# A batched matrix product in bf16: plain fp32 loads with casts on VectorE, stores on a second queue, long runs per partition

## The chip, the cores and the metric

The kernel runs on one core of a Trainium2 chip, with the other cores idle. Times are device microseconds of one execution. The profiled execution of the kernel before has a span of 276.1 us, while its timed executions have spans of 274.1 to 277.7 us (times 275.9 to 279.5), so it is one of its longer ones by about 1.7 us.

In the profiles PE is TensorE (matmuls), PEld its weight loads, DVE VectorE, ACT ScalarE, POOL GpSimd and SP SyncE; a q after a name is that engine's sequencer, which issues transfers and waits. SBUF is the on-chip memory with 128 partitions; PSUM takes the results of matmuls. A run is a piece of data that is contiguous in memory, and a packet is one record of a DMA engine's work.

## The reference

```python
batch, m, k, n = 16, 512, 768, 1024          # x: (16, 768, 512), y: (16, 768, 1024), fp32
np.einsum('bkm,bkn->bmn', x, y)              # out: (16, 512, 1024), fp32
```

It reads 75.5 MB and writes 33.55 MB, whatever the kernel does. Per batch, that is 4.72 MB in and 2.10 MB out.

## The kernel before

The load is a DMA on the GpSimd queue that casts fp32 to bf16 on its way. Row `ko*128 + p` of x or y goes to partition p, so a contiguous run is one row: 2 KB of x, 4 KB of y.

```python
x_v = x.rearrange("b (ko p) m -> b ko p m", p=P)
y_v = y.rearrange("b (ko p) n -> b ko p n", p=P)
o_v = out.rearrange("b (mo p) n -> b mo p n", p=P)
# x_pool, y_pool: 4 buffers; o_pool: 12; psum: 8 banks
for b in range(B):
    ...
    for c in range(LOAD_SPLIT):                       # two halves of the contraction
        ks = slice(c * KC, (c + 1) * KC)
        nc.gpsimd.dma_start(x_sb[:, ks], x_v[b, ks].rearrange("ko p m -> p ko m"))
        nc.gpsimd.dma_start(y_sb[:, ks], y_v[b, ks].rearrange("ko p n -> p ko n"))
    ...
    for kt in range(KT):                              # contraction outermost, 8 banks open
        for mt in range(MT):
            for nt in range(NT):
                mm(ps[mt * NT + nt], x_sb, y_sb, kt, mt, nt)
    for mt in range(MT):                              # copies alternate VectorE, ScalarE
        ...
        nc.sync.dma_start(o_v[b, mt], o_sb[mt][:])    # four stores of 512 KB
```

Of the kernel before, what the change touches and what calls it, by code (L numbers as in the profile page):

```python
# [1 line left out]

_os.environ.setdefault("NEURON_RT_ULTRASERVER_MODE", "4")

# [1 line left out]

# [4 lines left out]

LOAD_SPLIT = 2
K_OUTER = True


@with_exitstack
def kernel(
    ctx: ExitStack,
    tc: tile.TileContext,  # L20
    x: bass.AP,
    y: bass.AP,
    out: bass.AP,
):
    nc = tc.nc
    P = 128
    FP32 = mybir.dt.float32
    BF16 = mybir.dt.bfloat16

    B, K, M = x.shape  # L30
    _, _, N = y.shape

    KT = K // P
    MT = M // P
    NF = 512
    NT = N // NF
    KC = KT // LOAD_SPLIT

    x_v = x.rearrange("b (ko p) m -> b ko p m", p=P)
    y_v = y.rearrange("b (ko p) n -> b ko p n", p=P)  # L40
    o_v = out.rearrange("b (mo p) n -> b mo p n", p=P)

    x_pool = ctx.enter_context(tc.tile_pool(name="x_pool", bufs=4))
    y_pool = ctx.enter_context(tc.tile_pool(name="y_pool", bufs=4))
    o_pool = ctx.enter_context(tc.tile_pool(name="o_pool", bufs=12))
    psum = ctx.enter_context(tc.tile_pool(name="psum", bufs=8, space=bass.MemoryType.PSUM))

    def mm(ps, x_sb, y_sb, kt, mt, nt):
        nc.tensor.matmul(  # L49
            ps[:],  # L50
            x_sb[:, kt, mt * P:(mt + 1) * P],
            y_sb[:, kt, nt * NF:(nt + 1) * NF],
            start=(kt == 0),
            stop=(kt == KT - 1),
        )

    for b in range(B):
        x_sb = x_pool.tile([P, KT, M], BF16, name="x_sb")
        y_sb = y_pool.tile([P, KT, N], BF16, name="y_sb")
        for c in range(LOAD_SPLIT):  # L60
            ks = slice(c * KC, (c + 1) * KC)
            nc.gpsimd.dma_start(  # L62
                x_sb[:, ks], x_v[b, ks].rearrange("ko p m -> p ko m"))
            nc.gpsimd.dma_start(  # L64
                y_sb[:, ks], y_v[b, ks].rearrange("ko p n -> p ko n"))

        o_sb = [o_pool.tile([P, N], FP32, name="o_sb") for _ in range(MT)]
        ps = [psum.tile([P, NF], FP32, name="ps") for _ in range(MT * NT)]
        if K_OUTER:
            for kt in range(KT):  # L70
                for mt in range(MT):
                    for nt in range(NT):
                        mm(ps[mt * NT + nt], x_sb, y_sb, kt, mt, nt)
            for mt in range(MT):
                for nt in range(NT):
                    j = mt * NT + nt
                    eng = nc.vector.tensor_copy if j % 2 == 0 else nc.scalar.copy
                    eng(o_sb[mt][:, nt * NF:(nt + 1) * NF], ps[j][:])  # L78
                nc.sync.dma_start(o_v[b, mt], o_sb[mt][:])
        else:  # L80
            for mt in range(MT):
                for nt in range(NT):
                    j = mt * NT + nt
                    for kt in range(KT):
                        mm(ps[j], x_sb, y_sb, kt, mt, nt)
                    eng = nc.vector.tensor_copy if j % 2 == 0 else nc.scalar.copy
                    eng(o_sb[mt][:, nt * NF:(nt + 1) * NF], ps[j][:])
                nc.sync.dma_start(o_v[b, mt], o_sb[mt][:])


# [1 line left out]
_INS = ['x', 'y']  # L92
_OUTS = [((16, 512, 1024), 'float32')]


# [23 lines left out]
```

## Time and profile before

| | before |
|---|---|
| time, median | 276.1 us |
| PE busy | 192.3 us, 70% |
| DMA row of the page | 9 of 10 in all but the two ends |
| bytes at the source | 109.05 MB |
| from the last load's landing to the end of the span | 12.2 us |

The prediction below shows the page's lines. Here are the groups of instructions that the change touches. Columns: line, engine, operation, tiles, shapes, count; then busy us and mean ns of one; then the engine's idle time before them and what ended it.

```profile
L49 PE MATMUL ps<-y_sb,x_sb 128*128 128x512 bf16 x753 | 192.3, 416 | 77.0 <-DMA y_sb<-in_y_dram 72.3
L78 ACT COPY o_sb<-ps 128x512 f32<-128x512 f32 x64 | 32.9, 600 | 235.2 <-issue 172.9
L64 POOL DMA_DIRECT2D y_sb<-in_y_dram x32 | 24.7, 773 | 105.2 <-DMA y_sb<-in_y_dram 105.2
```

No engine but the DMA engines is full, and PE's idle time before matmuls ends with the landing of a load.

### The profile page before, as it was taken

The page shows a single profiled execution, that of the slowest core. Times are in us where ns is not written, and L with a number is a line of the kernel's source. Part 1 is how long each engine was busy: PE and PEld are TensorE (multiplying, and loading weights), DVE is VectorE, ACT ScalarE, POOL GpSimd, SP SyncE. Part 2 cuts the span into 40 slices and gives each one's busy share as a digit, 9 for nine tenths or more (in the row PEclk, how much of TensorE's full clock was granted, in tenths as well). Part 3 has the DMA queues.
Part 4 walks back from the last instruction along what each step waited for, and adds up shares of the span by engine and source line. Part 5 has one row for each costly group of instructions (what it writes and reads, how often), then busy time and mean ns, then how long its engine had stood idle before and what let it go on. Part 6 is the DMA issues. An engine that isn't in the chain of part 4 may idle for free.

```text
span 276.1 us, 2127 instructions
## 1 busy us (share of the span) xinstructions
PE 192.3 (70%) x753; PEld 79.9 (29%) x768; DVE 39.7 (14%) x64; ACT 34.1 (12%) x65; POOL 49.8 (18%) x68
## 2 busy tenths in 40 slices
PE   0599727698278788495784993769919695849770
PEld 0144313243133333132331441324403332313330
DVE  0003110033003003030300303003030030302011
ACT  1002110022002002020200202002020020202011
POOL 8422121221212122121212311122112221000000
PEclk9999977799689979889978898689986998997997
DMA  5999999999999999999999999999999999999937
GB/s 92 202 208 237 317 279 284 208 243 315 296 268 210 284 279 245 315 210 297 260 294 267 211 302 286 319 216 209 320 291 302 209 252 309 223 315 233 283 156 304
DMA packets 34826, 71.44 MB, mean 259 GB/s; under 512 B 2048, under 2 KB 14336, under 8 KB 34816
## 3 DMA queue, kind: packets, MB, share of 16 engines
q0 software_dynamic: 25600, 37.75, 75.7%
q1 hardware_dynamic: 9216, 33.56, 32.2%
q8 instruction: 6, 0.10, 0.1%
q14 instruction: 4, 0.03, 0.0%
HBM read 75.50 MB, written 33.55 MB: 395 GB/s over the span
## 4 chain that ended last, share of the span: by engine, by line
DMA 90%; issue 3%; POOL 2%; PE 2%; DVE 0%; DVEq 0%; POOLq 0%
DMA x_sb<-in_x_dram 78%; DMA y_sb<-in_y_dram 12%; PE ps L49 2%; POOL x_sb L62 1%; POOL y_sb L64 1%; DVE o_sb L78 0%; DVEq L114 0%; DVEq L78 0%; POOLq L114 0%; POOLq L103 0%
## 5 line engine op out<-in xcount | busy, mean ns | idle before, releaser
L49 PE MATMUL ps<-y_sb,x_sb 128*128 128x512 bf16 x753 | 192.3, 416 | 77.0 <-DMA y_sb<-in_y_dram 72.3
L49 PEld LDWEIGHTS <-x_sb 128*128 128x128 bf16 x768 | 79.9, 105 | 188.8 <-issue 109.9
L78 DVE COPY o_sb<-ps 128x512 f32<-128x512 f32 x64 | 39.7, 683 | 230.6 <-issue 167.7
L78 ACT COPY o_sb<-ps 128x512 f32<-128x512 f32 x64 | 32.9, 600 | 235.2 <-issue 172.9
L64 POOL DMA_DIRECT2D y_sb<-in_y_dram x32 | 24.7, 773 | 105.2 <-DMA y_sb<-in_y_dram 105.2
L62 POOL DMA_DIRECT2D x_sb<-in_x_dram x32 | 24.8, 777 | 76.5 <-DMA x_sb<-in_x_dram 70.7
L78 ACT ACT_TABLE_LOAD x1 | 1.3, 1283 | 0.7 <-PEq L103 0.7
L103 POOL MEMSET const-float32-0.0<- 128x1 f32 x1 | 0.1, 93 | 0.2 <-issue 0.2
L103 POOL MEMSET const-bfloat16-1.0<- 128x1 bf16 x1 | 0.1, 95 | 0.0
L103 POOL MEMSET const-float32-1.0<- 128x1 f32 x1 | 0.1, 93 | 0.0
L103 POOL MEMSET const-uint8-127<- 128x1 uint8 x1 | 0.1, 93 | 0.0
## 6 DMA issues: line engine op xcount, KB each, us to landing
out_dram<-o_sb SPq DMA_DIRECT2D x64, 512.0 KB, 8.9
y_sb<-in_y_dram POOLq DMA_DIRECT2D x32, 768.0 KB, 32.9
x_sb<-in_x_dram POOLq DMA_DIRECT2D x32, 384.0 KB, 32.8
```

The costliest lines, as they stand in the source:

```text
L49: nc.tensor.matmul(ps[:], x_sb[:, kt, mt * P:(mt + 1) * P], y_sb[:, kt, nt * NF:(nt + 1) * NF], start=(kt == 0), stop=(kt == KT - 1),)
L62: nc.gpsimd.dma_start(x_sb[:, ks], x_v[b, ks].rearrange("ko p m -> p ko m"))
L64: nc.gpsimd.dma_start(y_sb[:, ks], y_v[b, ks].rearrange("ko p n -> p ko n"))
L78: eng(o_sb[mt][:, nt * NF:(nt + 1) * NF], ps[j][:])
L103: nc = _bacc.Bacc("TRN2", target_bir_lowering=False, num_devices=1)
```

## The change

The intent is to take the cast off the DMA and GpSimd off the loads: plain copies on a hardware queue, with rows so long that each partition reads one contiguous piece. Row `p*6 + ko` now goes to partition p, so a run is 12 KB of x and 24 KB of y; output row `p*4 + mo` makes a store run 16 KB. VectorE casts from a staging buffer, and ScalarE alone empties PSUM. The order of instructions is fixed by hand (`tc.manual_schedule()`), and x and y have 2 bf16 buffers instead of 4. The diff, cut to its core:

```diff
-    x_v = x.rearrange("b (ko p) m -> b ko p m", p=P)
-    y_v = y.rearrange("b (ko p) n -> b ko p n", p=P)
-    o_v = out.rearrange("b (mo p) n -> b mo p n", p=P)
+    x_v = x.rearrange("b (p ko) m -> b p ko m", ko=KT)
+    y_v = y.rearrange("b (p ko) n -> b p ko n", ko=KT)
+    o_v = out.rearrange("b (p mo) n -> b p mo n", mo=MT)
...
+    def store(b):
+        nc.scalar.dma_start(o_v[b], o_tiles.pop(b)[:])
...
-            nc.gpsimd.dma_start(x_sb[:, ks], ...)     # two halves, cast in the DMA
-            nc.gpsimd.dma_start(y_sb[:, ks], ...)
+            nc.sync.dma_start(xs[:], x_v[b])          # fp32, staging, 2 buffers
+            nc.sync.dma_start(ys[:], y_v[b])
+            if False:
+                store(b - LAG)                        # LAG = 4, switched off
...
+            nc.vector.tensor_copy(x_sb[:], xs[:])
+            for h in range(2):
+                ks = slice(h * KT // 2, (h + 1) * KT // 2)
+                nc.vector.tensor_copy(y_sb[:, ks], ys[:, ks])
+            x_w = x_sb[:].rearrange("p k (j mo) -> p k mo j", mo=MT)   # weights stepped by 4
...
+            for mo in range(MT):                      # contraction innermost
+                for nt in range(NT):
+                    for kt in range(KT):
+                        nc.tensor.matmul(ps[:], x_w[:, kt, mo], y_sb[:, kt, ns], ...)
+                    nc.scalar.copy(o_sb[:, mo, ns], ps[:])
+            if True:
+                store(b)                              # one store of 2 MB
```

## The prediction

> **What bounds the kernel now.** I read the page first (busy shares, DMA row, queues, chain), then the chain in order of time, then windows, then the timeline of the end.
>
> ```profile
> PE 192.3 (70%) x753; PEld 79.9 (29%) x768; DVE 39.7 (14%) x64; ACT 34.1 (12%) x65; POOL 49.8 (18%) x68
> ...
> DMA  5999999999999999999999999999999999999937
> ...
> q0 software_dynamic: 25600, 37.75, 75.7%
> q1 hardware_dynamic: 9216, 33.56, 32.2%
> ...
> HBM read 75.50 MB, written 33.55 MB: 395 GB/s over the span
> ...
> DMA 90%; issue 3%; POOL 2%; PE 2%; DVE 0%; DVEq 0%; POOLq 0%
> ```
>
> The DMA row shows 9 in 37 of 40 slices, the chain that ended last is 90% DMA, and the largest engine, PE, is busy for 70%. The kernel is bound by the 16 DMA engines for all but its two ends. q0 counts 37.75 MB because the page counts bytes at the destination, which is bf16 for loads; the source read 75.50 MB.
>
> At what rate do they run? Windows (engine columns first; granted clock, DMA share and GB/s at the end of a row):
>
> ```profile
> 48.00:58.00 10.00, 7.50 (x27) 3.06 (x27) 1.95 (x4) 1.73 (x4) 2.32 (x3) 0.83 1.17 209
> 28.00:32.00 4.00, 2.73 (x13) 1.27 (x13) 0.00 (x0) 0.00 (x0) 0.77 (x1) 1.00 1.10 330
> ...
> 4.00:264.00 260.00, 187.10 (x731) 77.75 (x746) 37.24 (x60) 30.80 (x60) 46.80 (x61) 0.89 1.12 265
> ...
> 264.00:276.00 12.00, 5.18 (x23) 2.14 (x22) 2.48 (x4) 2.05 (x4) 0.00 (x0) 0.87 0.52 206
> ```
>
> At 48 to 58 only loads run: 209 GB/s of bf16 landed is 418 GB/s of fp32 read. At 28 to 32 stores take the larger part. Over 4 to 264 us 265 x 260 = 68.9 MB landed; 37.75 of it is loads, so 31.15 MB is stores, and counted at the source 75.5 + 31.15 = 106.65 MB moved in 260 us, 410 GB/s. If loads cost what they cost alone, they take 75.5 / 0.418 = 180.6 us, leaving 79.4 us for 31.15 MB of stores, 392 GB/s. So the engines have no idle time to win, only rate: 418 for loads in rows of 2 and 4 KB, 392 for stores in rows of 4 KB.
>
> The end is the other term:
>
> ```profile
> 230.94 32.91 DMA y_sb<-in_y_dram
> 263.85 0.04 issue
> 263.89 2.53 PE ps L49 x11
> ...
> 263.89 5.34 PE L49 MATMUL ps<-y_sb,x_sb 128*128 128x512 bf16 x23 [3.08 <-DMA y_sb<-in_y_dram]
> ...
> 268.63 2.88 SPq L79 DMA_DIRECT2D out_dram<-o_sb  x4
> ```
>
> The last load lands at 263.85. Only half a batch, 24 matmuls, is left (5.34 us, 222 ns each), the copies follow with the last groups, and the first of four stores is issued at 268.63. From the last landing to the end it is 276.1 - 263.9 = 12.2 us. From the packet records, those four stores' packets begin 1.6 us after the first issue and move their 2.1 MB in 5.2 us.
>
> **What the Trainium skill says.** "DMA: Bandwidth & Descriptors", section Measured: one 16 MB load reaches 425 GB/s on a core alone, and section Where 436 GB/s comes from: 435 GB/s is the ports' ceiling. The trace agrees so far as 418 and 392 both lie below it. The same page, section Why small descriptors are slow: each packet carries a fixed overhead on the engine's internal bus. The trace hints at it: a 4 KB store row takes 4096 / (392/16) = 167 ns of one engine, against 151 ns at 435/16. "VectorE: DVE Perf Modes", section The perf-mode tier table: an fp32 copy of 2048 columns in SBUF takes 1227 ns, two results a cycle; nothing in this trace shows it, as VectorE here only reads PSUM (683 ns for 512 columns). "TensorE: Matmul & The Clock Gate", section Weight-path perf modes: the fast weight load stays available with a column step from -1,023 to 1,024; the changed kernel steps by 4. The trace shows only step 1, at 105 ns.
>
> **The change, part by part.**
>
> 1. Loads move from GpSimd with a cast to 32 plain loads on SP. The 64 GpSimd issues (49.5 us busy in all) vanish, but none but the first was on a path that mattered, since DMA was busy throughout: 0 us. HBM traffic is unchanged, 75.5 + 33.55 = 109.05 MB. A partition's rows become 12, 24 and (stores) 16 KB in one run instead of 2 and 4 KB. I expect the per-packet loss nearly to vanish: about 427 GB/s for everything, an estimate between the skill's 425 for one long load and its ceiling of 435.
>
> 2. Are the engines kept fed? A load of batch b+2 waits for the casts of b, about 5 us after b lands, while b+1 (4.72 MB, at least 11 us) is still queued. In the compiled order some loads also wait for a store's shared semaphore, one that belongs to a batch five earlier, long landed. So no gap.
>
> 3. VectorE casts: three of 128x3072 per batch; at the skill's rate 3072/2 cycles at 0.96 GHz plus the 160 ns left over of 1227: 1.76 us each, 5.3 us per batch. At one result a cycle it would be 3.4 us each, 10 us per batch. A batch lasts 6.82 MB / 0.427 = 16 us, so both lie beside the DMA, except in the last batch.
>
> 4. Copies all on ScalarE: 8 x 600 ns = 4.8 us per batch, beside the matmuls. PE: 48 x 222 ns = 10.7 us, some 12 with cold stretches (446 ns each after idle of 4.9 us in this trace), under 16. Both off the path but for the last batch.
>
> 5. The last batch is the cost. y is now one load per batch, not two halves, so all 48 matmuls wait for it, with its two casts ahead; the 2.1 MB store is one transfer after all eight copies. From the last landing: two casts 3.5 (three matmuls fit beside the second), 45 matmuls x 222 = 10.0, cold start 0.8, last copy with its waits 0.9, issue 0.3, first byte 1.6, 2.1 MB at 420 GB/s 5.0, closing 0.7: 22.8 us, against 12.2.
>
> Sum: the first load issues at about 0.9 and flows by 2.7 us. When the last load lands, 14 stores have gone: store 14 is issued about one batch (casts 3.5, matmuls 11.5, copy 0.7) after its load, just as load 15 lands. So 75.5 + 14 x 2.097 = 104.9 MB / 0.427 = 245.7 us; 2.7 + 245.7 = 248.4 for the last landing, 15.5 us earlier than now. Plus 22.8 gives 271.2, a little under 2% faster. The change wins about 15 us of rate and gives 10.6 back in the end. I write 271.5.
>
> **The rivals.**
>
> A: the rate does not rise. If the hardware cuts a long run back into 4 KB packets, loads stay near 418 and stores near 392, mix 410: 104.9 / 0.410 = 255.9, total 281, 2% slower. For it: the engines are already at 94% of the ceiling. Against it: stores and loads differ, and the stores' 16 ns a row is what a fixed packet cost looks like.
>
> B: PE becomes the bound. Weights stepped by 4 columns may load more slowly. [...]At 300 ns the batch takes 14.4 us, still hidden, and only the end pays 3.5 us: 275. At 430 ns it takes 20.6 us, and 16 of them plus 14 us of start give some 350. The present pitch of 222 ns with loads of 98 to 105 leaves room of a factor two; I give the slow form 4%.
>
> C: everything goes well: 432 GB/s (242.8 us), warm PE, first store bytes sooner: 267.
>
> D: VectorE casts at one result a cycle: only the end pays, 3.3 us: 275.
>
> **Range and chances.** Each 5 GB/s is 2.9 us. 420 to 432 GB/s spans 276 to 268 with the end as computed; the end itself may be off by 3 us either way. Two per cent faster is 270.6, which lies beside my centre and needs 428 or a shorter end; 2% slower is 281.6, which needs A in full, or B. I say 266 to 281, faster 0.43, same 0.48, slower 0.09.
>
> **What will show it.** Step 1: rows of 12 to 24 KB on both hardware queues, and packets of that size; a window in mid-kernel at 420 to 432 GB/s (now bytes landed equal bytes read). 4 KB packets at 400 to 410 would be A. Step 2: the DMA row at 9 from the second slice to about the 37th, and the SP issues never the last to be waited for by the engines. Step 3: the cast rows at about 1.76 us. Step 4: weight loads at 100 to 150 ns and a warm matmul pitch near 222; PE idle a few us in each batch waiting for VectorE. Step 5: last landing near 248 and some 23 us from there to the end, with DMA idle for part of it. The prediction is wrong if the mid-kernel rate is outside 415 to 435, if the DMA row has holes, or if the end differs from 23 us by more than 4.

## The result, and the profile after

The changed kernel takes 272.49 us (271.82 to 273.49, four runs) beside 276.17 us. The ratio is 0.9862 (0.9828 to 0.9895), so it is 1.4% faster. A ratio here is the mean time of one kernel's runs over that of the other's of the same rounds, so it is not quite the ratio of the medians. Executions over 1.5% slower than the fastest of the same kernel are left out of the means.

The page after: busy shares, the DMA row with its rates in 40 slices, the queues, the total and the chain.

```profile
PE 197.6 (73%) x768; PEld 89.8 (33%) x768; DVE 83.0 (31%) x48; ACT 76.4 (28%) x129; POOL 0.2 (0%) x4
...
DMA  7999999999999999999999999999999999996507
GB/s 290 421 446 419 433 349 439 421 435 444 417 438 428 430 433 438 429 418 447 419 438 421 434 442 410 451 424 439 422 426 430 422 441 436 430 434 268 237 0 309
...
q1 hardware_dynamic: 4608, 75.50, 65.6%
q10 hardware_dynamic: 2304, 33.56, 29.0%
...
HBM read 75.50 MB, written 33.55 MB: 402 GB/s over the span
...
DMA 82%; DVE 10%; PE 4%; DVEq 1%; SPq 0%; issue 0%; ACT 0%
```

The middle runs at 410 to 450 GB/s; bytes landed are now bytes read. The new thing is at the right: the DMA row ends 6 5 0 7. One slice of 6.8 us moves nothing at all.

Only loads run from 5 to 24 us in both kernels. The windows, first of the kernel before, then of the changed one:

```profile
5.00:24.00 19.00, 13.95 (x56) 6.08 (x58) 2.48 (x4) 2.05 (x4) 7.28 (x11) 1.00 1.15 205
```

```profile
5.00:24.00 19.00, 7.60 (x22) 3.02 (x23) 6.95 (x4) 1.76 (x3) 0.00 (x0) 1.00 1.02 437
```

205 GB/s of bf16 landed are 410 GB/s read; the changed kernel reads 437. (A window counts a packet where it starts, so a long packet can carry it a little past the true rate; single microseconds of the packet records give 430 to 433.)

The groups after, for the casts, the copies and PE:

```profile
L74 PE MATMUL ps<-y_sb,x_sb 128*128 128x512 bf16 x768 | 197.6, 420 | 65.8 <-DVE y_sb L65 65.8
L74 PEld LDWEIGHTS <-x_sb 128*128 128x128 bf16 x768 | 89.8, 119 | 173.1 <-issue 54.0
L76 ACT COPY o_sb<-ps 128x512 f32<-128x512 f32 x128 | 75.2, 587 | 186.8 <-PE ps L74 186.8
L65 DVE CAST y_sb<-ys 128x3072 bf16<-128x3072 f32 x32 | 54.9, 1757 | 140.0 <-DMA ys<-in_y_dram 140.0
```

The end of the chain in order of time (start, us, what), and the same stretch in windows:

```profile
221.17 28.02 DMA ys<-in_y_dram
...
249.28 1.76 DVE y_sb L65
251.04 1.68 DVEq L106
...
252.76 10.61 PE ps L74 x45
...
263.40 0.59 ACT o_sb L76
```

```profile
252.00:256.00 4.00, 3.81 (x14) 1.55 (x13) 0.71 (x1) 0.96 (x2) 0.00 (x0) 0.72 0.66 274
256.00:260.00 4.00, 4.00 (x21) 2.08 (x19) 0.00 (x0) 1.88 (x4) 0.00 (x0) 1.00 0.00 0
260.00:264.00 4.00, 3.36 (x16) 1.55 (x14) 0.00 (x0) 1.86 (x4) 0.00 (x0) 1.00 0.00 0
264.00:268.00 4.00, 0.00 (x0) 0.00 (x0) 0.00 (x0) 0.00 (x0) 0.00 (x0) 0.99 0.84 356
```

The last load lands at 249.2. Two casts, 45 matmuls and a copy follow one after the other. The store of the batch before is done by about 256, and then the DMA engines stand still until the last 2 MB are ready at 264.

From the packet records I worked out, for every run, the stretch from the first load packet to the last, the rate in it, the stores still to do at its end, and how long no DMA engine worked after it. Times are medians of the fast runs; all other columns are of one execution. This table carries the rest of the document.

| run (profiled execution) | first to last load, us | GB/s in it | stores left, MB | after it, us | of that no DMA at all, us | time, us |
|---|---|---|---|---|---|---|
| kernel before | 260.5 | 408 | 2.8 | 11.5 | 3.6 | 276.2 |
| changed kernel | 247.0 | 424 | 4.2 | 21.2 | 10.6 | 272.5 |
| e1_short_rows | 256.8 | 408 | 4.2 | 22.1 | 11.4 | 284.3 |
| e2_short_loads | 258.1 | 406 | 4.2 | 22.5 | 12.2 | 285.3 |
| e3_short_stores | 238.5 | 424 | 8.0 | 20.8 | 0.0 | 264.2 |
| e7_before_long_loads | 253.0 | 416 | 3.8 | 11.5 | 1.3 | 270.3 |
| e4_one_queue | 243.0 | 425 | 5.7 | 22.4 | 6.9 | 270.2 |
| e5_last_stores | 245.8 | 426 | 4.3 | 18.7 | 7.3 | 269.9 |
| e6_short_end | 247.0 | 424 | 4.2 | 15.5 | 3.1 | 267.5 |
| f3_packets_4k | 249.3 | 418 | 4.8 | 21.0 | 7.4 | 273.2 |
| f4_packets_8k | 243.1 | 426 | 5.5 | 22.5 | 7.6 | 270.2 |
| f5_padded | 239.9 | 425 | 7.2 | 21.1 | 0.3 | 265.8 |
| f1_lag4 | 232.8 | 427 | 9.7 | 24.3 | 0.0 | 261.9 |
| f2_lag4_short_end | 232.8 | 426 | 9.9 | 24.4 | 0.0 | 262.2 |

Here the change won 13.5 us of stream (260.5 to 247.0) and gave back 9.7 us after the last load (11.5 to 21.2). What is left, 3.8 us, and loads that start 1.1 us earlier (1.7 instead of 2.85 us) make the 5.0 us between the two spans. The times differ by 3.7, because the profiled execution of the kernel before was one of its longer ones.

### The profile page after: what moved, and what is told of

It reads as the page before. It is cut to its first block, busy times and chain, and to the rows that moved or that the text cites. A ratio compares the mean times of both kernels' runs of the same rounds, so it can differ in the third digit from the quotient of the medians.

```text
span 271.1 us, 1889 instructions
## 1 busy us (share of the span) xinstructions
PE 197.6 (73%) x768; PEld 89.8 (33%) x768; DVE 83.0 (31%) x48; ACT 76.4 (28%) x129; POOL 0.2 (0%) x4
## 4 chain that ended last, share of the span: by engine, by line
DMA 82%; DVE 10%; PE 4%; DVEq 1%; SPq 0%; issue 0%; ACT 0%
DMA ys<-in_y_dram 82%; DVE y_sb L65 10%; PE ps L74 4%; DVEq L106 1%; SPq L56 0%; ACT o_sb L76 0%; SPq L57 0%; DVEq L65 0%
## 5 line engine op out<-in xcount | busy, mean ns | idle before, releaser
L74 PE MATMUL ps<-y_sb,x_sb 128*128 128x512 bf16 x768 | 197.6, 420 | 65.8 <-DVE y_sb L65 65.8
L74 PEld LDWEIGHTS <-x_sb 128*128 128x128 bf16 x768 | 89.8, 119 | 173.1 <-issue 54.0
L76 ACT COPY o_sb<-ps 128x512 f32<-128x512 f32 x128 | 75.2, 587 | 186.8 <-PE ps L74 186.8
L65 DVE CAST y_sb<-ys 128x3072 bf16<-128x3072 f32 x32 | 54.9, 1757 | 140.0 <-DMA ys<-in_y_dram 140.0
L62 DVE CAST x_sb<-xs 128x3072 bf16<-128x3072 f32 x16 | 28.2, 1760 | 29.7 <-DMA xs<-in_x_dram 28.6
```

The costliest lines, as they stand in the source:

```text
L62: nc.vector.tensor_copy(x_sb[:], xs[:])
L65: nc.vector.tensor_copy(y_sb[:, ks], ys[:, ks])
L74: nc.tensor.matmul(ps[:], x_w[:, kt, mo], y_sb[:, kt, ns], start=(kt == 0), stop=(kt == KT - 1))
L76: nc.scalar.copy(o_sb[:, mo, ns], ps[:])
```

## The experiments

All twelve gave right results and were timed in three rounds beside the kernel before. The first four ask where the rate comes from.

**Short rows again, on the new queues.**

```diff
-    x_v = x.rearrange("b (p ko) m -> b p ko m", ko=KT)      # y alike
-    o_v = out.rearrange("b (p mo) n -> b p mo n", mo=MT)
+    x_v = x.rearrange("b (ko p) m -> b p ko m", p=P)
+    o_v = out.rearrange("b (mo p) n -> b p mo n", p=P)
-            x_w = x_sb[:].rearrange("p k (j mo) -> p k mo j", mo=MT)
+            x_w = x_sb[:].rearrange("p k (mo j) -> p k mo j", mo=MT)
```

> The changed kernel with the old addressing: loads in rows of 2 KB (x) and 4 KB (y), stores in rows of 4 KB, still plain loads on SP and stores on ACT. Theory (the length of the run sets the rate): the rates of the kernel before come back, 418 GB/s for loads and 392 for stores, so 75.5/0.418 + 29.4/0.392 = 255.6 us up to the last landing against 104.9/0.431 = 243.4 in the changed kernel; the end stays at 22 us, so about 284 to 286 us, slower than before by 3%. Rival (the plain hardware-queue load without cast is what is faster, not the run): the rate stays near 430 and the time near 272.

Measured: 284.33 us, ratio 1.0257. The window of loads alone, in this run:

```profile
5.00:24.00 19.00, 6.80 (x19) 2.53 (x20) 6.95 (x4) 1.17 (x2) 0.00 (x0) 1.00 1.03 405
```

The plain hardware-queue load with short rows reads 405 GB/s, no more than the casting load of the kernel before. In mid-kernel, where loads run alone, it is slower: 399 (74 to 80 us), where the kernel before reads 418 (48 to 58, in the prediction). The rival falls: the queue and the missing cast bring nothing in sum (408 GB/s in both streams), and with the longer end the kernel is 2.6% slower than before. That the time met the band of 284 to 286 is in part luck: the loss was to come from loads and stores both, and the next two runs show more of it on the loads and next to none on the stores.

**Only the loads short.**

```diff
-    x_v = x.rearrange("b (p ko) m -> b p ko m", ko=KT)      # y alike
+    x_v = x.rearrange("b (ko p) m -> b p ko m", p=P)
```

> Only the loads go back to rows of 2 and 4 KB; stores keep 16 KB. Theory (run length): load-only windows near 418 GB/s, cost 75.5 x (1/0.418 - 1/0.431) = 5.4 us, so about 278. Rival (loads gain from the queue, not from the run): 272.

Measured: 285.34 us, ratio 1.0289: 13 us over the changed kernel, not 5, and as slow as with both short. The expectation took 418 from the casting loads; plain loads in short rows read 399 (73 to 80 us, loads alone).

The packet records give the cost. On the hardware queues a packet takes, in the median, 86 to 87 ns for 2 KB, 159 to 160 for 4 KB, 309 for 8 KB, 460 for 12 KB, 611 for 16 KB and 912 for 24 KB. From 12 to 24 KB that is 27.2 bytes a ns (16 times this is 435 GB/s), and over every packet lie another 8 to 12 ns, for loads and for stores. As an estimate from these medians, the short loads take 12,288 x (87 + 160) / 16 = 189.7 us of the 16 engines' time and the long ones 2,048 x (460 + 912) / 16 = 175.6: 14 us, near the 13 measured.

**Only the stores short.**

```diff
-    o_v = out.rearrange("b (p mo) n -> b p mo n", mo=MT)
+    o_v = out.rearrange("b (mo p) n -> b p mo n", p=P)
-            x_w = x_sb[:].rearrange("p k (j mo) -> p k mo j", mo=MT)
+            x_w = x_sb[:].rearrange("p k (mo j) -> p k mo j", mo=MT)
```

> Only the stores go back to rows of 4 KB; loads keep 12 and 24 KB; weights are then read without a step. Theory (run length): cost 29.4 x (1/0.392 - 1/0.431) = 6.8 us, so about 279; together with the run with short loads it should add up to the run with both short. A second thing to read: weight loads should fall from 119 ns to about 105 if the step of 4 columns costs anything. Rival: 272.

Measured: 264.20 us in three runs, ratio 0.9534 (the fourth, 269.91, was slow). This contradicts both theory and rival: shorter stores made the kernel 8 us faster. Two readings of it. First, the stores' run length costs little: the stream runs at 424 GB/s as with long stores, and stores alone run at 424 (241 to 248 us), against 419 and 429 with 16 KB (the changed kernel and f1_lag4, 250 to 255 us). Against that, e1 and e2 both run near 407. So the loads' rows are what the rate depends on, by about 17 GB/s. Their length changed together with the order of their addresses in HBM, and no run separates the two for loads; the packet times above speak for the length, since 4 KB packets take the same time as loads and as stores, and as stores in either order (e3 and f5_padded below, both 159 ns). Second, the loads land 8.5 us sooner, with 8.0 MB of stores left instead of 4.2. The DMA row at the right end has no hole any more:

```profile
DMA  7999999999999999999999999999999999999977
```

Weight loads fell from 119 to 103 ns as expected of unstepped weights, but e1, which is also unstepped, is only 1 us faster than e2. PE is not on the path in mid-kernel.

**Long loads in the kernel before.**

```diff
-    x_v = x.rearrange("b (ko p) m -> b ko p m", p=P)        # y alike
+    x_v = x.rearrange("b (p ko) m -> b p ko m", ko=K // P)
-                x_sb[:, ks], x_v[b, ks].rearrange("ko p m -> p ko m"))
+                x_sb[:, ks], x_v[b][:, ks])
```

> The kernel before with one edit: its loads, still cast on the GpSimd queue, address runs of 6 KB (x) and 12 KB (y) per partition. Theory (run length, whatever the queue): load-only windows rise from 418 to about 430 GB/s of fp32 read (215 of bf16 landed), worth 5.4 us: about 271, with the short end kept. Rival (the cast on the software queue holds the loads at 418): 276.

Measured: 270.32 us, ratio 0.9756, as the theory said. The window of loads alone:

```profile
5.00:24.00 19.00, 14.30 (x58) 6.19 (x59) 2.48 (x4) 2.05 (x4) 4.32 (x9) 1.00 1.06 214
```

214 of bf16 are 428 GB/s read, from 410. With no staging, no cast on VectorE and the short end kept, four edited lines are worth more than the whole change. Long rows raise the loads' rate on the software queue too.

The next three ask about the end and the queues.

**Stores on the loads' queue, two batches later.**

```diff
-        nc.scalar.dma_start(o_v[b], o_tiles.pop(b)[:])
+        nc.sync.dma_start(o_v[b], o_tiles.pop(b)[:])
-            if False:
+            if b >= LAG:                                    # LAG = 2
                 store(b - LAG)
...
-            if True:
+            if False:
                 store(b)
```

> Stores moved to the loads' queue on SP, each issued two batches later so that its wait does not hold the loads back. Theory (all queues run on the same 16 engines; a second queue only saves issue time): rate near 430, time within 1% of the changed kernel's, 270 to 275 us. Rival (loads and stores on two queues overlap better): the mixed windows fall towards 400 to 410 and the time rises to 280 or more.

Measured: 270.22 us, ratio 0.9765; 425 GB/s in the stream. A second queue brings no bandwidth. That agrees with the Trainium skill, "DMA: Bandwidth & Descriptors", section Issuing engines are not separate DMA queues.

**The last store in four.**

```diff
                     nc.scalar.copy(o_sb[:, mo, ns], ps[:])
+                if b == B - 1:
+                    nc.scalar.dma_start(o_v[b][:, mo], o_sb[:, mo])
```

> Only the last batch's store is split in four, by output row, each issued when its two copies are done. Theory (the end is serial: casts, 45 matmuls, then 2.1 MB by itself): only 0.5 MB is left after the last copy, 1.2 us in place of 5.0, so 3.7 us less, about 268.5 to 269. Rival (the end is not what was given back; it lies behind something else): 272.

Measured: 269.88 us, ratio 0.9755: 2.6 us less by the medians and 3.5 by the profiled spans (271.1 and 267.6), where 3.7 was expected. The end is on the path, as the theory says. The packets after the last load take 18.7 us instead of 21.2.

**The last batch split as in the kernel before, and finer.** The edit, in words and core lines: y of the last batch in three loads, four casts, the contraction outermost over eight banks, copies on two engines, four stores.

```diff
+            cuts = [0, 2, 4, 6] if b == B - 1 else [0, KT]
+            for lo, hi in zip(cuts, cuts[1:]):
+                nc.sync.dma_start(ys[:, lo:hi], y_v[b][:, lo:hi])
...
+                for kt in range(KT):                        # last batch only
+                    for mo in range(MT):
+                        for nt in range(NT):
+                            nc.tensor.matmul(ps[mo * NT + nt][:], x_w[:, kt, mo], ...)
```

> The last batch alone is treated as the kernel before treated every batch, and finer: y in three loads of two row blocks each, casts of two, two, one and one row blocks, matmuls with the contraction outermost over eight banks, copies on both VectorE and ScalarE, four stores on SP. Theory: from the last landing to the end: cast 0.7, 16 matmuls 3.5, copy and issue 1.0, first byte 1.6, 2.1 MB 5.0 partly beside the copies, closing 0.7: 10 to 12 us in place of 22, so about 261 to 263, 5% faster than the kernel before. Rival (skew among the DMA engines or the backlog of the store before sets the end): 267 or more.

Measured: 267.54 us, ratio 0.9673. It is better than the changed kernel by 5 us, but my sum was off by another 5. The timeline shows why (start, us, engine, line, operation):

```profile
248.22 10.52 PE L87 MATMUL ps<-y_sb,x_sb 128*128 128x512 bf16 x48
...
249.19 1.29 DVE L68 CAST y_sb<-ys 128x1024 bf16<-128x1024 f32 x2 [1.22 <-DMA ys<-in_y_dram]
```

PE starts the last batch's 48 matmuls at 248.2, just before the last piece of y lands at 249.2. I had counted only 16 of them after the landing; but PE is busy with batch 14 until 248.2, because that batch too waited for its one load and its casts. Loading the last batch in pieces does not help while PE has not finished the batch before. The time lies in the rival's range of 267 or more, but not for its reason: the chain ends with 8.86 us of the last matmuls and the copies, and the DMA engines still have 3.1 us without work.

The last five runs ask why short stores were fast. The theory that I formed from e3: the engines take a packet from each queue in turn, so packet lengths set the shares. The packet records of the middle support it. In the changed kernel, in the microseconds in which only y packets of 24,576 bytes and store packets of 16,384 move (1.5 to 1), loads get 260 GB/s and stores 171 in the mean. In e3, with 24,576 against 4,096 (6 to 1), they get 363 and 67. With x packets of 12,288 bytes it is 186 to 243 (0.75 to 1) and 320 to 102 (3 to 1). In e2 it is the loads that have the small packets: 76 to 349. The Trainium skill, "DMA: Bandwidth & Descriptors", section Queues, rings and completion order, says that an engine goes round the queues that have work by packets; the traces agree, and a "packet" is here one contiguous run: from 78 to 104 us in the changed kernel, of 137 store packets whose successor can be told by its start time, 119 are followed by a load packet.

**Four transfers per store, packets of 4 KB.**

```diff
-        nc.scalar.dma_start(o_v[b], o_tiles.pop(b)[:])
+        o = o_tiles.pop(b)
+        for mo in range(MT):
+            nc.scalar.dma_start(o_v[b][:, mo], o[:, mo])
```

> The run with short stores was 8 us faster than the changed kernel where 7 us slower was expected. New theory: the engines take one packet from each queue in turn, so the packet sizes set the shares; with 24 KB load packets against 4 KB store packets the loads get 6/7 of the rate, land 8 us sooner, and the stores held back run in the time that the last batch's casts and matmuls leave idle. This kernel keeps the changed kernel's addresses and stepped weights and only cuts each store into four transfers of 4 KB packets. Theory: near 264 us, last landing 8 us sooner, no idle DMA after it. Rival (what helped was the unstepped weight read, or the other order of addresses in HBM): 272.

Measured: 273.22 us, ratio 0.9882. The theory seemed to fall. The waits of the load queue (who waited for what, total us, times, longest) tell what else had changed:

```profile
SPq L59 <- DMA out_dram<-o_sb: 124.4, 13, 20.6
SPq L58 <- DMA out_dram<-o_sb: 84.2, 12, 13.0
```

The compiled program has eight completion semaphores for its hardware-queue transfers (the traces name them), and a transfer waits for the one that used its semaphore before. With six transfers per batch, a load waits for a store three or four batches earlier (y of batch 15 for one of batch 12), so loads cannot run far ahead, and only 4.8 MB of stores are left when they end. In the changed kernel and in e3 it is a store five batches earlier, and in the changed kernel no such wait appears before the closing ones. In f3 the copies on ScalarE, whose queue issues the stores, also waited 42.6 us for stores. The run is confounded, not a refutation; which of these waits cost how much stays open.

**Two transfers per store, packets of 8 KB.**

```diff
-        nc.scalar.dma_start(o_v[b], o_tiles.pop(b)[:])
+        o = o_tiles.pop(b)
+        for mo in range(0, MT, 2):
+            nc.scalar.dma_start(o_v[b][:, mo:mo + 2], o[:, mo:mo + 2])
```

> The same with two transfers of 8 KB packets per store: loads of y get 3/4. Theory of shares: stores fall behind less than with 4 KB, last landing between the two, so between 264 and 268 us. Rival (only 4 KB packets or the addresses matter): 272.

Measured: 270.15 us, ratio 0.9758, outside the band of 264 to 268 and below the rival's 272. The last load lands 3.9 us sooner than in the changed kernel, but the stores kept up better than I had thought (5.5 MB left), so 7.6 us without any DMA remain.

**One store, padded in SBUF, packets of 4 KB.** This keeps the changed kernel's addresses, weights and number of transfers.

```diff
-            o_sb = o_pool.tile([P, MT, N], FP32, name="o_sb")
+            o_sb = o_pool.tile([P, MT, N + 16], FP32, name="o_sb")
-        nc.scalar.dma_start(o_v[b], o_tiles.pop(b)[:])
+        nc.scalar.dma_start(o_v[b], o_tiles.pop(b)[:, :, 0:N])
```

> The run with four transfers of 4 KB packets took 273 us, not 264; in its trace the loads' issues waited 209 us in all for stores, because more transfers share the same eight completion semaphores, so the loads could not run ahead. This kernel takes that confound away: one store per batch as in the changed kernel, same addresses in HBM and same stepped weights, but the output tile in SBUF is padded by 64 bytes per row so that a packet cannot be longer than 4 KB. Theory of shares: about 264 us, stores 7 to 9 MB behind at the last landing, no idle DMA time after it, as in the run with short stores. Rival (unstepped weights or the order of addresses made that run fast): 272. If loads are again held by stores' semaphores, 270 or more, and the SP waits will show it.

Measured: 265.81 us in the three fast runs (263.29 to 266.90; the fourth, 267.66, counted as slow), ratio 0.9556 (0.9431 to 0.9681); 0.3 us without DMA, 7.2 MB of stores left. The DMA row:

```profile
DMA  7999999999999999999999999999999999999947
```

The 4 is a slice in which some of the engines had run out of work and others had not.

It scatters more than the others. Packet length alone, with addresses, weights and number of transfers kept, gives most of e3's gain; unstepped weights and address order are not needed for it. The last clause of the expectation was wrong: here, and in e3, loads do wait for stores' semaphores (166 us in all), and the time is not 270. The engines work off stores meanwhile: in e3 they move 423 GB/s, stores alone, from 79.2 to 83.8 us.

**Stores on the loads' queue, four batches later**, with the LAG of 4 that stands unused in the changed kernel.

```diff
-        nc.scalar.dma_start(o_v[b], o_tiles.pop(b)[:])
+        nc.sync.dma_start(o_v[b], o_tiles.pop(b)[:])
-            if False:
+            if b >= LAG:
                 store(b - LAG)
...
-            if True:
+            if False:
                 store(b)
```

> Stores on the loads' queue on SP with 16 KB packets, each issued four batches later, so that store order is set by the program, not by shares. Theory (what counts is the DMA time left idle after the last load, 10.6 us in the changed kernel): 12 stores instead of 14 done at the last landing, 100.7 MB / 0.425 = 237 us, then 8.4 MB of stores beside 15 us of casts and matmuls: idle 1 to 3 us, time 262 to 265. Rival (one queue with a long lag blocks the loads): 270 or more.

Measured: 261.91 us (261.67 to 262.40), ratio 0.9474 (0.9445 to 0.9502). This holds stores back by program order, with 16 KB packets and no shares between queues, and has the same effect. From e4 it differs in the lag alone, four batches for two: 8.3 us. The DMA row and two windows of the end:

```profile
DMA  7999999999999999999999999999999999999994
```

```profile
248.00:252.00 4.00, 0.38 (x2) 0.00 (x0) 0.00 (x0) 0.59 (x1) 0.00 (x0) 1.00 0.99 422
252.00:256.00 4.00, 0.00 (x0) 0.00 (x0) 0.00 (x0) 0.00 (x0) 0.00 (x0) 0.63 0.99 426
```

The compute ends near 249, eleven microseconds before the span's end, and the engines still move 422 to 426 GB/s. This is 5.3% faster than the kernel before and 10.6 us faster than the changed one, by three edited lines. It is the best version found.

**Lag 4 and the short end together.** The two edits above in one, with the held-back stores issued ahead of the last batch's:

```diff
+                for c in sorted(o_tiles)[:-1]:              # last batch only
+                    store(c)
```

> As the run with lag 4, with the last batch split as in the run with the short end. Theory: no idle DMA time is left, so the span is 2.7 + 109.05/0.425 + 0.7 = 260 us and the time, which has been 1.9 us above the span for the changed kernel, about 262. If the lag alone already leaves no idle time, the two agree within 1 us. Rival (the end of PE's work sets the time): the same as the run with lag 4 minus 3 us or more.

Measured: 262.20 us, ratio 0.9482: the same as lag 4. When the DMA engines have no idle time after the last load, shortening the compute at the end is worth nothing. The e6 edit was worth 5 us where there was a hole, and 0 where there was none.

## Why the prediction was right

The time of 272.49 lies 1.0 us above the forecast of 271.5, in the range, and the outcome is in "same", the likeliest of the three by a little.

- **Step 1, rate.** Predicted about 427 GB/s, measured 424.5 over the stream and 430 to 432 in the middle half of the microseconds from 60 to 230. Against 431.5 the stream loses 4.0 us: 0.9 in its first 4 us, 1.3 in a dip from 32 to 38 us, when the first store starts, 1.2 in its last 3 us, where the last y load's 16 completions are spread from 245.3 to 248.8, and the rest in between. The last landing came at 249.2 instead of 248.4.
- **Step 1, its reason, was half right.** I put the loss on both loads (418) and stores (392) for their short rows. For loads this was shown, for run length and order of addresses together: e1 and e2 lose it, e7 gains it on the old queue. For stores it was wrong: 4 KB stores on the plain queue run at 424, alone as well as beside long loads. The number of 392 was a remainder of a division, and it carried more than row length. The fixed cost of a packet is there, but some 8 ns at 4 KB instead of the 16 read from that remainder. A 4 KB store packet took 172 ns in the kernel before and in e7, beside the software queue's casting loads, and 159 ns in e1, e3 and f5. And e1 has the 408 GB/s of the kernel before, although its loads alone are slower (399 against 418). So part of the gain came with the queue after all, through the stores. No run isolates this; that it is the software queue is argued, not shown.
- **Step 2, engines fed.** Right: the DMA row is 9 from the second slice to the 36th; its hole in the 39th is the idle time that step 5 foresaw.
- **Step 3, casts.** Predicted 1.76 us each, measured 1.757 and 1.760. The two results a cycle that the Trainium skill gives for an fp32 copy ("VectorE: DVE Perf Modes", section The perf-mode tier table) hold for the cast to bf16. Rival D falls.
- **Step 4, copies and PE.** Weight loads 119 ns, hidden; rival B falls. PE waits a few us per batch for VectorE, as said.
- **Step 5, the end.** Predicted 22.8 us, measured 271.1 - 249.2 = 21.9. The two casts took 3.44, the 45 matmuls 10.61 with their cold start (predicted 10.8), the copy 0.59, and the 2.1 MB 5.1. From the store's issue to its first packet it was 0.85, not 0.3 + 1.6: the 1.6 was misread, as on the span's clock the kernel before also has 0.8 (268.63 to 269.45). The closing took 1.2, not 0.7. That the end gives back most of the gain was the point of the sum, and e5 and e6 show that it is on the path.
- **Span and time.** I took 276.1 as both span and time. The profiled execution happened to have a span equal to the median time. The sum of 271.2 was a span; four runs of the changed kernel have spans of 269.8 to 271.6. Read so, the forecast was nearly exact; each time lies 1.9 to 2.1 us above its span. That a span, with only 0.3 us added, came within 1.0 us of the time is in part luck: the loads began 1.0 us earlier than assumed (1.7, not 2.7), their stream was 1.3 us longer, and the end 0.9 us shorter.

Rival A (packets cut back to 4 KB) falls: the records have packets of 12,288, 24,576 and 16,384 bytes. What the prediction did not ask is whether the end has to be idle. It took "14 stores have gone when the last load lands" as a fact of the schedule, and it was the largest lever of all: 10.6 us.

## What to carry to other kernels

When DMA is full in mid-kernel, ask two separate things: at what rate the engines run (here longer rows of the loads raised it, on either queue), and for how long they stand idle at the ends. After the last load there is always some compute; keep enough stores back to fill it, by issuing them some batches late or by giving the loads the longer packets. Before believing an experiment that adds transfers, look at what the load queue waits for: shared completion semaphores can undo the effect you want to see.

## What the Trainium skill lacked or had wrong

- "DMA: Bandwidth & Descriptors" advises that spreading transfers over queues does not help bandwidth. The runs agree (e4, 425 GB/s on one queue), but the page lacks that run lengths set each queue's share: 260 to 171 GB/s at 1.5 to 1, 363 to 67 at 6 to 1, and that this alone was worth 6 to 7 us (f5_padded against the changed kernel).
- The same page gives a packet as some 9 to 17 descriptors; in these traces the queues alternate by single contiguous runs of 4 to 24 KB (119 of 137 store packets, above).
- The same page has no comparison of row lengths for plain loads on a hardware queue: 405 GB/s with rows of 2 and 4 KB, 437 with 12 and 24 KB (windows of loads alone, 5 to 24 us). Nor has it the time of a long packet: 159 ns for 4 KB, 912 for 24 KB.
- No page has how long a store waits for its first packet beside running loads: 3.4 to 4.0 us from the issue for the first 14 stores of the changed kernel, 0.84 and 0.85 for the two issued after the last load.
- "TensorE: Matmul & The Clock Gate" says that stepped weights keep the fast load, but not what they cost: 119 ns in the mean with a step of 4, 103 ns without (e3_short_stores).
- "VectorE: DVE Perf Modes" has an fp32 copy but no cast in its tier table, and no page has a time for one: 1757 ns for 3072 columns of fp32 to bf16.
